# Moving 56 elementwise adds from VectorE to GpSimd in a one-core transformer layer

## The chip, the core and the metric

The kernel runs on one core of a Trainium2 chip. The engines are named as in the profile: PE (TensorE, matmul) with PEld (its weight loads), DVE (VectorE), ACT (ScalarE), POOL (GpSimd) and SP (SyncE, which here issues nearly all DMAs). Each engine executes its own instructions strictly in their order in the program, and waits on semaphores for the others. The metric is the device time of one execution in microseconds (us); lower is better.

## What is computed

One layer of a streaming encoder on `x` (2048 tokens of 1024 float32 values): a token mixer, cross-attention into 256 memory tokens, and a SwiGLU feed-forward net, each between two RMS norms and with a residual.

```python
u = rms_norm(h, g_mix_pre)
qa, ka, va, qh, fh, ih, gh = jnp.split(u @ w_in, IN_SPLITS, axis=-1)
y = jnp.concatenate([swa_with_sinks(qa, ka, va, sinks),        # sliding-window attention
                     hgrn2(qh, fh, ih, gh, lb, onorm)], -1) @ w_out
h = h + rms_norm(y, g_mix_post)
u = rms_norm(h, g_x_pre)
y = cross_attention(u, rms_norm(mem, g_mem), wq_x, wk_x, wv_x, wo_x)
h = h + rms_norm(y, g_x_post)
u = rms_norm(h, g_ffn_pre)
y = (jax.nn.silu(u @ w_gate) * (u @ w_up)) @ w_down
h = h + rms_norm(y, g_ffn_post)
```

## The kernel before, in words

**Products.** All float32 products are made of three matmuls each on operands split into a high and a low part: hi*hi, hi*lo, lo*hi (lines 1131 to 1133). The big products are in addition done by a seven-product scheme on 2x2 blocks (`seven`, steps 1, 5, 6, 3, 7, 2, 4). It needs sums and differences of the blocks of both operands. A token operand's blocks and sums are tiles named `S` (128x512) and `sum`; a weight operand's are tiles named `T`. Each is split by `split2`: the high part is copied by ACT (line 987) or by POOL (line 989), the low part is a subtraction on DVE (line 990) of two tiles in SBUF. A step of `seven` is 12 matmuls; `phases` makes the `S` two steps ahead, into five buffers.

**Sums of the weights ahead of time.** The four combined weight blocks of the chain (`CHAIN`, keys 5, 7, 6, 4) are made once, ahead of the stage that needs them, and kept in DRAM. `sums` (line 1418) makes the DRAM tile and a generator `combined` (line 1027), which for two halves of the inner dimension loads two blocks of 128x1024, lets three steps go by, adds or subtracts them on DVE (line 1034) and stores the result. That is 8 adds for each weight. They run beside the stage before: `out_s` (sums of `w_out`) beside the sliding-window attention (line 228), `qk_s` beside the out projection, `vo_s` beside the scores, `u_s` and `d_s` in the feed-forward net. The tiles come from small pools: `u` and `x` (2 and 3 buffers) for `out_s`, one `extra` tile with `row` or `gain` tiles for the others.

**Stages, in order of time.** The input projection; the sliding-window attention with the HGRN recurrence and the rest of the input projection between them (`swa`, `hgrn`, `in_proj`); the folding of the cross-attention weights into a query-key matrix `qk_d` and a value-output matrix `vo_d`; then `phases` over the jobs of `jobs` (line 1441): the out projection (`mixed_block`), the scores (`score_block`), the values (`value_block`), then gate, up and down of the feed-forward net. Each of the first three jobs has 8 blocks of 256 tokens.

**What follows a block.** `mixed_block` and `value_block` have an `after` generator that is drawn a little at each of the following steps. In `mixed_block` (line 1539): the reciprocal norm on POOL (`rstds`, lines 1515 to 1519, three tiny instructions), a scaling on DVE (line 1557), the residual add of the rows of `x` (line 1558, two of 128x1024 for a block), the store of the new rows, squares on ACT (line 1504), another reciprocal norm, and transposes on DVE (line 1398). `value_block` is alike: scaling (1630), residual add of the rows of `h1_d` (1634, two for a block), store, squares, reciprocal norm, scaling (1643), transposes on PE (1390). In `score_block` POOL makes a tiny product `x_mr` (line 1590) for each half row, which ACT's exponentials (line 1592) wait for.

**The order of the work** on each engine is fixed when the program is built: the scheduler places the instructions by priority and by its own timeline, and each engine then keeps to that order. `behind()` ties the instructions traced in it behind the last marked ones of ACT and DVE, each only on that same engine.

Of the kernel before, what the change touches and what calls it, by code (L numbers as in the profile page):

```python
# [15 lines left out]
ALU = mybir.AluOpType  # L16
# [32 lines left out]
class Layer:  # L49
# [144 lines left out]
    def mix(self):  # L194
        tc, I = self.tc, self.I
        kw = dict(reuse_waits="tile")
        with contextlib.ExitStack() as left:
            def pool(name, at, **k):
                return at.enter_context(tc.tile_pool(name=name, bufs=1, **k, **kw))

            self.mc = pool("mc", left)
            self.r_x = self.cst.tile([P, NT], F32, name="r_x")
            with (
                tc.tile_pool(name="t1", bufs=3, **kw) as self.ts,
                tc.tile_pool(name="t2", bufs=3, **kw) as self.tb,
                tc.tile_pool(name="s1", bufs=2, side="right", **kw) as self.st_pool,
                contextlib.ExitStack() as at,
            ):
                self.banks(at, "ps1", **MOST)
                self.raws = 3  # L210
                u = self.in_first()
            self.banks(left, "ps2", **FOUR)
            self.hg = pool("hg", left)
            self.wp = pool("wp", left)
            self.io = pool("io", left)
            with tc.tile_pool(name="sw", bufs=1, side="right", **kw) as self.sw:
                self.zero_tiles()
                swa = self.swa(range(NT), lambda n: "st" if n < NPB else "sth")
                hgrn = self.hgrn(range(NPB), "h")
                cols = self.in_proj(1, u)  # L220
                next(cols)
                for _ in range(NPB + 1):
                    next(swa)
                    next(hgrn)
                    next(cols)
                for _ in hgrn:
                    pass
                self.out_sums, side = self.sums("out_s", self.w_out, 4, lambda: self.io_tile("u"), lambda: self.io_tile("x"))
                side = side()
                next(side)  # L230
                pairs = self.hgrn(range(NPB, NT), "gt")
                for i, _ in enumerate(swa, NPB + 2):
                    next(cols)
                    if i == NT + 1 - 0:
                        next(pairs)
                    for _ in range(4):
                        next(side, None)
                for _ in cols:
                    pass
            phases = self.phases(self.jobs(), None, lambda: self.io_tile("z"))  # L240
            with tc.tile_pool(name="xp", bufs=1, side="right", **kw) as self.xp:
                fold = self.fold_cross()
                for _ in range(2):
                    next(fold)
                for i, _ in enumerate(pairs, 1):
                    for _ in range(2):
                        next(fold)
                    if 2 <= i < 10:
                        next(phases)
                for _ in fold:  # L250
                    pass
            left.close()
            with (
                tc.tile_pool(name="t3", bufs=3, **kw) as self.ts,
                tc.tile_pool(name="t4", bufs=3, **kw) as self.tb,
                tc.tile_pool(name="s3", bufs=2, side="right", **kw) as self.st_pool,
                contextlib.ExitStack() as at,
            ):
                self.banks(at, "ps3", **MOST)
                self.raws = 4  # L260
                for _ in phases:
                    pass
# [761 lines left out]
                keep[key] = src  # L1024
            yield lambda a=a, b=b, t=t, o=o: split(a, b, t, o)

    def combined(self, get, nk, dst):

        nc = self.nc
        halves = [(0, (nk + 1) // 2), ((nk + 1) // 2, nk)]  # L1030
        for a, b in halves:
            def put(key, t, o, op):
                with self.behind():
                    nc.vector.tensor_tensor(t, t, o, op)
                self.store(dst[self.CHAIN.index(key), :, a * 512:b * 512], t.rearrange("p k d -> p (k d)"))

            for x, y, key in (((0, 1), (0, 0), 5), ((1, 1), (0, 1), 7), (None, (0, 0), 6), (None, (1, 0), 4)):
                if x:
                    t = get(0, *x, a, b - a)
                o = get(1, *y, a, b - a)  # L1040
                for _ in range(3):
                    yield
                if key == 4:
                    put(4, o, t, ALU.subtract)
                else:
                    put(key, t, o, ALU.add if key == 6 else ALU.subtract)
                yield
# [367 lines left out]
            p = P if i else 64  # L1415
            self.load(d, self.I["w_out"][r:r + p * n, j * 512:(j + 1) * 512].rearrange("(k p) d -> p k d", p=p))

    def sums(self, name, src, nk, *tiles):

        dst = self.tc.dram_tile([4, P, nk * 512], F32, name=name)  # L1420

        def get(which, i, j, k0, n):
            t = tiles[which]().rearrange("p (k d) -> p k d", d=512)[:, :n]
            src(t, i, j, k0, n)
            return t

        return dst, lambda: self.combined(get, nk, dst)

    def token_sums(self, a, o, n):

# [10 lines left out]
    def jobs(self):  # L1441
        I = self.I

        def weights(src, r0, nk):
            return lambda t, i, j, k0, n: self.load(
                t, src[r0 + (i * nk + k0) * P:r0 + (i * nk + k0 + n) * P, j * 512:(j + 1) * 512]
                .rearrange("(k p) d -> p k d", p=P))

        def ffn_u(b):
            return lambda t, i, j, k0, n: self.load(  # L1450
                t, self.u_d[4 * i + k0:4 * i + k0 + n, :, b * TB + j * 512:b * TB + (j + 1) * 512]
                .rearrange("k p t -> p k t"))

        def kinds(blocks, n=0, last="p"):
            return [("p" if i < n else last if i == len(blocks) - 1 else "s",) + b for i, b in enumerate(blocks)]

        def sums(name, src, nk, other=None):
            return self.sums(name, src, nk, self.extra_tile, other or self.gain_tile)

        def in_turn(*what):  # L1460
            return lambda: itertools.chain.from_iterable(w() for w in what)

        qk, vo = weights(self.qk_d, 0, 4), weights(self.vo_d, 0, 4)
        down = [(weights(I["w_down"], f0 * P, nk), f0, nk) for f0, nk in ((0, 3), (6, 4), (14, 4))]
        qk_s, vo_s = sums("qk_s", qk, 4, self.row_tile), sums("vo_s", vo, 4)
        u_s = sums("u_s", ffn_u(1), 4)
        self.u0_s = self.tc.dram_tile([4, P, 4 * 512], F32, name="u0_s")
        d_s = [sums(f"d_s{c}", src, nk) for c, (src, _, nk) in enumerate(down)]
        jobs = [(self.w_out, 4, kinds([self.mixed_block(n) for n in range(0, NT, 2)], 1), self.out_sums, {1: [qk_s[1]]}),
                (qk, 4, kinds([self.score_block(n) for n in range(0, NT, 2)]), qk_s[0], {1: [vo_s[1]]}),  # L1470
                (vo, 4, kinds([self.value_block(n) for n in range(0, NT, 2)]), vo_s[0], {})]
        for b in range(NB):
            beside = {2: [in_turn(*(d[1] for d in d_s))]} if b else {4: [u_s[1]]}
            jobs.append((ffn_u(b), 4, kinds([blk for f in range(0, NFF, 2) for blk in self.hidden_blocks(b, f)], 0, "s"),
                         u_s[0] if b else self.u0_s, beside))
        for c, (src, f0, nk) in enumerate(down):
            jobs.append((src, nk, kinds([self.down_block(c, f0, nk, n) for n in range(0, NT, 2)], 0, "s"), d_s[c][0], {}))

        return jobs
# [59 lines left out]
    def mixed_block(self, n):  # L1539
        nc = self.nc  # L1540
        y, x, ss = {}, [], []
# [11 lines left out]
        def after():  # L1553
            r = self.rstds(ss[0])
            s2 = self.small("q_s", 4)
            for i in range(2):
                nc.vector.scalar_tensor_tensor(y[i], y[i], r[:, i:i + 1], self.g_mix_post, ALU.mult, ALU.mult)
                nc.vector.tensor_tensor(y[i], y[i], x[i], ALU.add)
                self.store(self.h1_d[(n + i) * P:(n + i + 1) * P, :], y[i])
                yield  # L1560
            yield
# [48 lines left out]
    def value_block(self, n):  # L1610
        nc = self.nc
        y, ss, u, o = {}, [], {}, {}
# [12 lines left out]
        def after():  # L1625
# [5 lines left out]
            yield  # L1631
            yield
            for i in range(2):
                nc.vector.tensor_tensor(y[i], y[i], x[i], ALU.add)
                self.store((self.out if n < NT - 2 else self.h2_d)[(n + i) * P:(n + i + 1) * P, :], y[i])
                yield
            for i in range(2):
# [153 lines left out]
```

## Time and profile before

| | |
|---|---|
| median of 3 runs | 2554.41 us (2552.43 to 2555.48) |
| the profiled execution | 2550.01 us, its span 2548.3 us |
| PE busy | 2504.8 us, 98% |
| PEld busy | 2092.8 us, 82% |
| DVE busy | 1792.1 us, 70% |
| ACT busy | 1261.6 us, 50% |
| POOL busy | 364.6 us, 14% |
| mean granted clock of PE | 0.997 |

Times in the views are counted from the start of the span. Busy time is the time in which an instruction of the engine was running. An instruction that stands in its engine's queue and waits for a semaphore counts as idle; the views name in brackets what ended such a wait. Matmuls overlap each other, so the listed 390 ns of one is longer than the distance of two.

### The profile page before, as it was taken

How to read it: one execution, taken by the hardware profiler on the slowest of the kernel's cores; microseconds unless marked ns; L12 is line 12 of the kernel's file. 1: busy time of each engine (PE TensorE's matmuls, PEld its weight loads, DVE VectorE, ACT ScalarE, POOL GpSimd, SP SyncE). 2: the span in 40 equal slices, each digit the busy share in tenths (PEclk: the TensorE clock that was granted, in tenths of full speed). 3: DMA queues.
4: the chain of work that ended last, by engine and by line, in shares of the span. 5: the costliest groups of instructions: out<-in, count | busy, mean ns of one | idle time of the engine just before them, and what ended most of it. 6: DMA issues, size and time to landing. Idle time of an engine off the chain costs nothing.

```text
span 2548.3 us, 34324 instructions
## 1 busy us (share of the span) xinstructions
PE 2504.8 (98%) x12006; PEld 2092.8 (82%) x12006; DVE 1792.1 (70%) x2871; ACT 1261.6 (50%) x2635; POOL 364.6 (14%) x540
## 2 busy tenths in 40 slices
PE   9999999999999999999999999999999999999998
PEld 8878888877997778878878888888888888878886
DVE  8885488987556989988876555576566557574766
ACT  5553466655555566566753333353333335443543
POOL 4231234321311112102200000000000000000022
PEclk9999999999999999999999999999999999999999
DMA  6455655865887996867954522254465434564786
GB/s 201 146 165 178 192 154 170 230 204 146 259 292 275 316 335 189 274 206 226 333 200 146 177 91 87 74 203 148 160 210 195 144 117 159 180 188 106 228 177 151
DMA packets 387885, 486.33 MB, mean 191 GB/s; under 512 B 22272, under 2 KB 283392, under 8 KB 387712
## 3 DMA queue, kind: packets, MB, share of 16 engines
q1 hardware_dynamic: 381664, 462.12, 55.9%
q0 software_dynamic: 6048, 22.02, 5.0%
q8 instruction: 94, 1.54, 0.2%
q14 instruction: 79, 0.65, 0.1%
HBM read 317.34 MB, written 166.72 MB: 190 GB/s over the span
## 4 chain that ended last, share of the span: by engine, by line
PE 51%; DVE 2%; DMA 1%; issue 1%; ACT 1%; POOL 0%; SPq 0%; DVEq 0%; POOLq 0%; ACTq 0%
PE psm L1133 17%; PE psm L1131 17%; PE psm L1132 17%; DVE T L990 0%; DVE S L990 0%; ACT junk L1504 0%; PE pss L1390 0%; DMA out_dram<-row 0%; DMA row<-d_s 0%; DMA row<-in_w_down_dram 0%; DMA u_d<-row 0%; DMA sraw<-in_w_gate_dram 0%; DVE sum L1106 0%; ACT S L987 0%; ACT T L987 0%
## 5 line engine op out<-in xcount | busy, mean ns | idle before, releaser
L1131 PE MATMUL psm<-T,S 128*128 128x512 f32 x2680 | 1034.1, 390 | 13.3 <-ACT part L1146 7.2
L1132 PE MATMUL psm<-T,S 128*128 128x512 f32 x2680 | 1042.3, 390 | 4.0 <-DVE T L990 3.9
L1133 PE MATMUL psm<-T,S 128*128 128x512 f32 x2680 | 1029.4, 389 | 4.1 <-DVE S L990 4.1
L1131 PEld LDWEIGHTS psm<-T,S 128*128 128x128 f32 x2680 | 503.0, 188 | 125.9 <-ACT part L1146 11.9
L1132 PEld LDWEIGHTS psm<-T,S 128*128 128x128 f32 x2680 | 503.2, 188 | 110.5 <-DVE T L990 7.3
L1133 PEld LDWEIGHTS psm<-T,S 128*128 128x128 f32 x2680 | 503.1, 188 | 110.6 <-DVE S L990 6.3
L987 ACT ACTIVATE S<-sum 128x512 fp32r<-128x512 f32 (+1 forms) x370 | 224.0, 620 | 371.5 <-PE psm L1133 267.3
L990 DVE TENSOR_TENSOR S<-sraw,S 128x512 fp32r<-128x512 f32 (+1 forms) x315 | 211.5, 679 | 218.8 <-ACT S L987 215.8
L1146 ACT ACTIVATE part<-psm 128x512 f32<-128x512 f32 x285 | 168.6, 596 | 251.9 <-PE psm L1133 230.9
L990 DVE TENSOR_TENSOR S<-sum,S 128x512 fp32r<-128x512 f32 (+1 forms) x388 | 257.4, 673 | 42.1 <-ACT S L987 38.3
L987 ACT ACTIVATE S<-sraw 128x512 fp32r<-128x512 f32 (+1 forms) x300 | 184.7, 618 | 110.8 <-PE psm L1133 106.0
L1537 POOL DMA_DIRECT2D y_d<-row x16 | 14.1, 879 | 1077.9 <-DVE row L1721 1027.6
L990 DVE TENSOR_TENSOR T<-row,T 128x1024 fp32r<-128x1024 f32 (+1 forms) x112 | 131.0, 1183 | 30.2 <-ACT T L987 29.2
L157 PE MATMUL psg<-u,whi 128*128 128x512 f32 x320 | 128.3, 401 | 0.0
L158 PE MATMUL psg<-u,wlo 128*128 128x512 f32 x320 | 127.6, 399 | 0.0
L156 PE MATMUL psg<-u,whi 128*128 128x512 f32 x320 | 127.5, 399 | 0.0
L1504 ACT ACTIVATE junk<-row 128x512 f32<-128x512 f32 x160 | 99.6, 624 | 40.6 <-DVE row L1526 20.6
L987 ACT ACTIVATE T<-row 128x1024 fp32r<-128x1024 f32 (+1 forms) x112 | 113.3, 1031 | 7.5 <-DMA row<-d_s 4.3
L1672 DVE TENSOR_TENSOR row<-psm,part 128x512 f32<-128x512 f32 x66 | 43.7, 687 | 66.9 <-PE psm L1133 66.9
L1681 DVE TENSOR_TENSOR part<-psm,part 128x512 f32<-128x512 f32 x66 | 43.8, 687 | 60.1 <-PE psm L1133 59.8
L1721 DVE TENSOR_TENSOR row<-psm,part 128x512 f32<-128x512 f32 x72 | 49.1, 688 | 49.5 <-PE psm L1133 49.4
L814 ACT ACTIVATE S<-S,w_mn 128x256 f32<-128x256 f32 (+1 forms) x128 | 63.0, 496 | 29.6 <-DVE w_mn L810 29.2
(363 smaller groups left out, 3562.2 us busy)
## 6 DMA issues: line engine op xcount, KB each, us to landing
sraw<-in_w_gate_dram SPq DMA_DIRECT2D x44, 512.0 KB, 3.6
sraw<-in_w_up_dram SPq DMA_DIRECT2D x44, 512.0 KB, 3.7
hid_d<-row SPq DMA_DIRECT2D x44, 512.0 KB, 2.7
sraw<-hid_d SPq DMA_DIRECT2D x32, 512.0 KB, 4.2
sraw<-in_w_in_dram SPq DMA_DIRECT2D x44, 256.0 KB, 4.0
z_d<-pair SPq DMA_DIRECT2D x20, 512.0 KB, 3.4
raw<-in_w_in_dram SPq DMA_DIRECT2D x20, 512.0 KB, 4.8
z_d<-z SPq DMA_DIRECT2D x20, 512.0 KB, 4.0
```

The source lines that it names most:

```text
L156: nc.tensor.matmul(ps, ah, bh, start=(i == 0), stop=False)
L157: nc.tensor.matmul(ps, ah, bl, start=False, stop=False)
L158: nc.tensor.matmul(ps, al, bh, start=False, stop=(i == n - 1))
L814: nc.scalar.activation(s[:, r, o:], s[:, r, o:], AF.Exp, bias=mn[:, i:i + 1], scale=-1.0, accum_out=den[:, i:i + 1])
L987: self.nc.scalar.activation(hi, raw, AF.Copy)
L990: self.nc.vector.tensor_tensor(lo, raw, f32(hi), ALU.subtract)
L1131: nc.tensor.matmul(ps, s[:, 0, k, :], t[:, 0, k, :], start=st, stop=False, **kw)
L1132: nc.tensor.matmul(ps, s[:, 0, k, :], t[:, 1, k, :], start=False, stop=False, **kw)
L1133: nc.tensor.matmul(ps, s[:, 1, k, :], t[:, 0, k, :], start=False, stop=sp, **kw)
L1146: nc.scalar.activation(t, ps, AF.Copy)
L1504: self.nc.scalar.activation(junk, a, AF.Square, scale=float(D) ** -0.5, accum_out=to)
L1721: nc.vector.tensor_tensor(d, a, b, ALU.add)
```

## The change

Three groups of adds, 56 instructions of 128x1024 each, are issued on POOL instead of DVE:

- line 1558, the residual of the out projection: 16 adds
- line 1634, the residual of the values: 16 adds
- line 1034, for `out_s`, `qk_s` and `vo_s`: 8 adds each, 24

The sums `u_s` and `d_s` stay on DVE. No operand, no tile and no load is changed.

```diff
-                self.out_sums, side = self.sums("out_s", self.w_out, 4, lambda: self.io_tile("u"), lambda: self.io_tile("x"))
+                self.out_sums, side = self.sums("out_s", self.w_out, 4, lambda: self.io_tile("u"), lambda: self.io_tile("x"),
+                                                 on=self.nc.gpsimd)
...
-    def combined(self, get, nk, dst):
+    def combined(self, get, nk, dst, on):
...
                 with self.behind():
-                    nc.vector.tensor_tensor(t, t, o, op)
+                    on.tensor_tensor(t, t, o, op)
...
-        return dst, lambda: self.combined(get, nk, dst)
+        return dst, lambda: self.combined(get, nk, dst, on or self.nc.vector)
...
-        qk_s, vo_s = sums("qk_s", qk, 4, self.row_tile), sums("vo_s", vo, 4)
+        qk_s, vo_s = sums("qk_s", qk, 4, self.row_tile, on=self.nc.gpsimd), sums("vo_s", vo, 4, on=self.nc.gpsimd)
...
-                nc.vector.tensor_tensor(y[i], y[i], x[i], ALU.add)
+                nc.gpsimd.tensor_tensor(y[i], y[i], x[i], ALU.add)
                 self.store(self.h1_d[(n + i) * P:(n + i + 1) * P, :], y[i])
...
-                nc.vector.tensor_tensor(y[i], y[i], x[i], ALU.add)
+                nc.gpsimd.tensor_tensor(y[i], y[i], x[i], ALU.add)
                 self.store((self.out if n < NT - 2 else self.h2_d)[(n + i) * P:(n + i + 1) * P, :], y[i])
```

More of the change, by code (lines that the diff above doesn't have):

```diff
@@ L1025, in resident @@
             yield lambda a=a, b=b, t=t, o=o: split(a, b, t, o)
-    def combined(self, get, nk, dst):
-        nc = self.nc
+    def combined(self, get, nk, dst, on):
         halves = [(0, (nk + 1) // 2), ((nk + 1) // 2, nk)]
@@ L1416, in w_out, with sums @@
             self.load(d, self.I["w_out"][r:r + p * n, j * 512:(j + 1) * 512].rearrange("(k p) d -> p k d", p=p))
-    def sums(self, name, src, nk, *tiles):
+    def sums(self, name, src, nk, *tiles, on=None):
         dst = self.tc.dram_tile([4, P, nk * 512], F32, name=name)
@@ L1455, in kinds, with sums @@
             return [("p" if i < n else last if i == len(blocks) - 1 else "s",) + b for i, b in enumerate(blocks)]
-        def sums(name, src, nk, other=None):
-            return self.sums(name, src, nk, self.extra_tile, other or self.gain_tile)
+        def sums(name, src, nk, other=None, **at):
+            return self.sums(name, src, nk, self.extra_tile, other or self.gain_tile, **at)
         def in_turn(*what):
```

## The prediction, made before the changed kernel ran

> **What bounds the kernel now.** I read the page's first part, then the busy time of the stages in which adds are moved (each row gives the stretch, then busy time of PE, PEld, DVE, ACT and POOL with the instructions counted, clock, DMA share and GB/s).
>
> ```profile
> PE 2504.8 (98%) x12006; PEld 2092.8 (82%) x12006; DVE 1792.1 (70%) x2871; ACT 1261.6 (50%) x2635; POOL 364.6 (14%) x540
> ```
>
> ```profile
> 440.00:526.00 86.00, 84.73 (x465) 71.42 (x464) 77.02 (x165) 52.43 (x140) 28.73 (x40) 1.00 0.86 249
> 800.00:955.00 155.00, 149.31 (x649) 120.75 (x647) 138.69 (x177) 96.51 (x211) 25.61 (x50) 1.00 0.93 311
> 955.00:1105.00 150.00, 148.88 (x655) 122.81 (x655) 140.42 (x264) 92.02 (x218) 27.38 (x36) 1.00 0.79 238
> 1105.00:1300.00 195.00, 187.03 (x864) 151.90 (x865) 164.96 (x206) 129.13 (x277) 31.67 (x48) 1.00 0.78 261
> ```
>
> PE is the bound everywhere. In these four stages (attention with `out_s`, out projection, scores, values) it idles 86.00 - 84.73 = 1.27, then 5.69, 1.12 and 7.97 us: 16.1 us together. No change of DVE's work can win more than that. DVE is the busiest helper: 90%, 89%, 94% and 85% of these stages, so it has 9.0, 16.3, 9.6 and 30.0 us of idle time left.
>
> Next, whom PE waited for. First the waits of PE in the out projection, then in the scores, then in the values (sum, times, longest):
>
> ```profile
> PE psm L1133 <- DVE S L990: 1.4, 2, 1.2
> PE psm L1132 <- DVE T L990: 0.6, 1, 0.6
> ```
>
> ```profile
> PE psm L1132 <- DVE T L990: 1.4, 1, 1.4
> ```
>
> ```profile
> PE psm L1133 <- DVE S L990: 2.7, 2, 1.6
> PE psm L1132 <- DVE T L990: 1.9, 4, 0.8
> ```
>
> So 8.0 us of PE's idle time end with a low part that DVE made late. That is what the change can remove, and also what it can make longer.
>
> **What is removed from DVE.** The groups by line and shape, cut to the stages (count | busy, mean ns | idle before them and what ended it):
>
> ```profile
> L1034 DVE TENSOR_TENSOR u<-u,x 128x1024 f32<-128x1024 f32 x6 | 7.3, 1214 | 3.0 <-DMA out_s<-u 2.8 <-issue 0.3
> ```
>
> ```profile
> L1558 DVE TENSOR_TENSOR row<-row,row 128x1024 f32<-128x1024 f32 x16 | 19.1, 1216 | 0.0
> L1034 DVE TENSOR_TENSOR extra<-extra,row 128x1024 f32<-128x1024 f32 x6 | 7.3, 1213 | 3.0 <-issue 1.9 <-DMA qk_s<-extra 1.1
> ```
>
> ```profile
> L1034 DVE TENSOR_TENSOR extra<-extra,g 128x1024 f32<-128x1024 f32 x6 | 7.3, 1216 | 3.3 <-DMA extra<-vo_d 3.3
> ```
>
> ```profile
> L1634 DVE TENSOR_TENSOR row<-row,row 128x1024 f32<-128x1024 f32 x16 | 19.1, 1217 | 0.0
> ```
>
> Of the 24 sums these rows show 18; the other 6 have the same shape. 56 adds of 1.217 us are 68 us of DVE. Instructions on DVE overlap a little (16 take 19.1 us), so one costs its queue 1.13 to 1.20 us; in a row of two I count 1.13 (2.35 for both, below). Besides, 3.0 + 3.0 + 3.3 = 9.3 us go in which DVE stood at the head of its queue waiting for the load of a sum. Nearly all of this lies beside PE's work and is worth nothing. One wait is not. First DVE, then PE:
>
> ```profile
> 881.41 1.22 DVE L1034 TENSOR_TENSOR extra<-extra,row 128x1024 f32<-128x1024 f32 x1 [1.08 <-DMA qk_s<-extra]
> 882.55 0.68 DVE L1106 TENSOR_TENSOR sum<-sum,sraw 128x512 f32<-128x512 f32 x1
> 883.15 0.68 DVE L990 TENSOR_TENSOR S<-sraw,S 128x512 fp32r<-128x512 f32 x1
> ```
>
> ```profile
> 883.89 0.50 PE L1133 MATMUL psm<-T,S 128*128 128x512 f32 x1 [1.25 <-DVE S L990]
> ```
>
> Without the add, its 1.08 us of waiting and its 1.13 us go from ahead of `S`, 2.2 us against PE's 1.25: **-1.25 us**. Next late there is ACT, which waits for PE itself.
>
> **What the same add costs on POOL.** No POOL add of 128x1024 is in the trace; the nearest row is one of half the size with two inputs (minimum, median, maximum in ns):
>
> ```profile
> L914 POOL TENSOR_TENSOR W<-W,G x16: 1042/1046/2005, 254.2 to 717.1; 128x512 f32<-128x512 f32 x16
> ```
>
> So about 2 x 1.04 = 2.1 us alone (estimate; its ends are the 1.04 of half the size and 4.0, twice the maximum). POOL has the time: 56 x 2.1 = 118 us against some 470 idle in these stages. But why is the maximum 2005? POOL, then DVE, around that instruction:
>
> ```profile
> 359.32 2.00 POOL L914 TENSOR_TENSOR W<-W,G 128x512 f32<-128x512 f32 x1
> ```
>
> ```profile
> 358.15 2.33 DVE L734 TENSOR_TENSOR_SCAN u<-reset,x 128x512 f32<-128x512 f32 x2
> 360.52 1.36 DVE L771 SCALAR_TENSOR_TENSOR qs<-qd,qs 64x512 fp32r<-64x512 f32 x1
> ```
>
> ```profile
> L771 DVE SCALAR_TENSOR_TENSOR qs<-qd,qs x32: 687/690/1579, 275.0 to 581.9; 64x512 fp32r<-64x512 f32 x32
> ```
>
> The scans (two inputs in SBUF) end at 360.48, and POOL's add, issued at 359.32, ends at 361.32: it worked 0.84 us after them. DVE's next instruction, also with two SBUF inputs, takes 1.36 instead of 0.69: it stood 0.67 us until POOL let go. They exclude each other. For twice the length I take 2 x 0.84 = 1.7 us during which DVE stands (1.3 from 2 x 0.67, 2.1 from the whole duration). Where DVE works without a pause on two-input instructions, an add on POOL thus costs DVE 1.7 instead of 1.13: **0.57 us more, not 1.13 less** (0.2 to 1.0). Where DVE has a pause or reads PSUM, the 1.13 are won, mostly where PE does not wait.
>
> [...]
>
> **Where that meets a wait of PE.** (1) The end of the out projection:
>
> ```profile
> 950.79 1.22 DVE L1558 TENSOR_TENSOR row<-row,row 128x1024 f32<-128x1024 f32 x1
> 951.93 1.22 DVE L990 TENSOR_TENSOR T<-row,T 128x1024 fp32r<-128x1024 f32 x1
> 953.06 0.69 DVE L990 TENSOR_TENSOR S<-sraw,S 128x512 fp32r<-128x512 f32 x1
> 953.66 1.22 DVE L1558 TENSOR_TENSOR row<-row,row 128x1024 f32<-128x1024 f32 x1
> 954.80 1.22 DVE L990 TENSOR_TENSOR T<-row,T 128x1024 fp32r<-128x1024 f32 x1
> ```
>
> ```profile
> 953.20 0.50 PE L1132 MATMUL psm<-T,S 128*128 128x512 f32 x1 [0.55 <-DVE T L990]
> 956.07 0.50 PE L1132 MATMUL psm<-T,S 128*128 128x512 f32 x1 [1.44 <-DVE T L990]
> ```
>
> DVE has no pause and nearly all of it has two inputs. Two adds stand ahead of the `T` that PE waits for: 2 x 0.57 = **+1.1 us** (between -2.0, if POOL gets its turn only after that `T`, and +2.0).
>
> (2) The values, where token sums follow the residual. SP, DVE, PE:
>
> ```profile
> 1196.47 1.48 SPq L78 DMA_DIRECT2D out_dram<-row  x2
> ...
> 1199.82 0.67 SPq L78 DMA_DIRECT2D u_d<-row  x1
> ```
>
> ```profile
> 1195.22 2.35 DVE L1634 TENSOR_TENSOR row<-row,row 128x1024 f32<-128x1024 f32 x2
> ...
> 1206.44 0.69 DVE L1432 TENSOR_TENSOR row<-row 128x512 f32<-128x512 f32 x1 [2.26 <-DMA u_d<-row]
> ```
>
> ```profile
> 1211.40 0.50 PE L1133 MATMUL psm<-T,S 128*128 128x512 f32 x1 [1.63 <-DVE S L990]
> ```
>
> SP stands at the stores of the rows until the adds are done (1196.4 and 1195.22 + 2.35 = 1197.57), then comes to the store of `u_d`; DVE's token sum waits for that store to land, and the `S` behind it makes PE wait. On POOL the second add ends about 1.8 us later (start at 1195.3 after the `S` that DVE has in hand, 1.7, up to 0.7 for a DVE instruction between, 1.7 = 1199.4): **+1.8 us**. In the changed program three more stores precede that `u_d` store, but one `S` less stands behind the token sum; so I keep 1.8, between -1.6 (the wait gone) and +5. This is the queue where the move counts most: every residual store has SP's next `sraw` load behind it, but those loads are for the block after (a block takes 150 / 8 = 19 us), so a shift of 2 us is hidden there; without that cover it would be 2 us for each of 16 blocks.
>
> (3) The last block of the values:
>
> ```profile
> 1288.68 0.50 PE L1132 MATMUL psm<-T,S 128*128 128x512 f32 x1 [0.47 <-DVE T L990]
> ```
>
> Right ahead of that `T` DVE does one residual add: **+0.6 us**. In the other pairs PE does not wait on DVE, and DVE's pauses take the excess.
>
> (4) On POOL's own queue stand, behind an add that waits for its load: the three tiny norm instructions, the high parts of some weights, and in the scores `x_mr`, for which ACT waits already (in that stage from 1000 on):
>
> ```profile
>   ACT row L1592: 20.9, 11
> ```
>
> ACT's copies of `S` queue behind those exponentials. But `S` is made two steps ahead, 24 matmuls of 148.88 / 655 = 0.227 us, that is 5.4 us, and PE idles almost nowhere in that stage. Cost 0; without the cover 7 adds x 2.1 us = 15. In the attention I cost the exchange at 0 as well: PE idles 1.27 us there, half of DVE's work reads PSUM, and the scheduler reorders all engines (-1 to +2).
>
> **The sum.** -1.25 + 1.1 + 1.8 + 0.6 = +2.3 us: 2550.0 + 2.3 = 2552.3 us for the profiled execution. The median before is 2554.41, 4.4 us above that execution, so the forecast is **2556.7 us**, 0.1% slower. A measurement of this kernel can tell about 0.2% (5.1 us) from no change: that is 2549.3 to 2559.5.
>
> **Rivals.** *DVE's relief decides.* POOL takes its adds in DVE's pauses, and the waits on DVE's `S` and `T` go: -8.0 us and about 1 in the attention, **2545.4 us**. For it: 65 us of DVE's idle time in the four stages and the 9.3 us of head-of-queue waits. Against it: 56 adds want 95 us of exclusive access, and where PE waits there are no pauses. Chance 0.21.
>
> *The exclusion decides (slower).* In the out projection DVE is at 89%, and 24 adds each take 0.57 us more of it: 13.7 us against 16.3 us idle. Much of that idle time is DVE waiting for PE or ACT, so it can't be used. If nearly every grant to POOL meets a ready two-input instruction, DVE bounds that stage: +13.7 - 1.25 = 12.4, **2566.8 us**. It decides as soon as more than about half of the grants do so. [...] Chance 0.19.
>
> *POOL's queue decides (slower).* `x_mr` or the high part of a weight comes late behind adds that wait for loads: half of the 14.6 us above, **about 2562 us**. Chance 0.15.
>
> That the change does not do what it says is excluded: the built program has 56 more instructions on POOL, on just these lines.
>
> **How the numbers follow.** Forecast 0.45, rivals 0.21, 0.19 and 0.15. Faster by over 0.2%: 0.21; within: 0.45; slower: 0.34. The range goes from the first rival to the second, 2545 to 2567.
>
> **What would show it.** The 56 adds on POOL at about 2.1 us, up to 3 where DVE is busy; DVE instructions with two SBUF inputs at up to 1.7 us above their 0.69 or 1.22 beside them, those with a PSUM input unchanged; no wait before 883.9, longer ones at the end of the out projection and at the token sums. Wrong would be: PE's idle time in the four stages under 11 us or above 24, or a PE wait on something that stands behind POOL.

## The result: 2.2% slower, and the profile after

The changed kernel takes 2610.43 us (median of 4 runs, 2606.12 to 2611.78), the kernel before in the same session 2554.36 (2552.43 to 2555.48): ratio 1.0221, 95% interval 1.0208 to 1.0233. The forecast was 2556.7 us, with a range of 2545 to 2567. The profiled execution takes 2609.64 us (span 2607.9, granted clock 0.990 instead of 0.997).

First the page's busy times after the change:

```profile
PE 2525.1 (97%) x12006; PEld 2103.6 (81%) x12006; DVE 1825.5 (70%) x2815; ACT 1257.3 (48%) x2635; POOL 532.6 (20%) x596
```

Two things are odd here. DVE has lost 56 adds (68 us) and is busy 33 us *longer* than its 1792.1. And PE, with the same 12006 matmuls, is busy 20.3 us longer than its 2504.8. Now the four stages, cut at the same matmuls as in the prediction (stretch, its length, then busy time of PE, PEld, DVE, ACT, POOL, and the granted clock):

```profile
438.20:532.90 94.70, 87.96 (x464) 73.91 (x463) 75.55 (x164) 53.42 (x146) 45.75 (x51) 0.96 0.84 222
812.90:988.80 175.90, 156.59 (x649) 124.71 (x648) 158.84 (x155) 95.21 (x210) 98.69 (x73) 0.95 0.82 268
988.80:1152.50 163.70, 155.12 (x657) 125.61 (x655) 141.98 (x252) 91.24 (x218) 50.78 (x46) 0.97 0.72 220
1152.50:1360.80 208.30, 191.32 (x867) 154.19 (x866) 179.27 (x189) 128.73 (x276) 84.48 (x64) 0.98 0.76 248
```

Against 86, 155, 150 and 195 us the stages are 8.7, 20.9, 13.7 and 13.3 us longer, 56.6 in all. PE's idle time in them is 6.7, 19.3, 8.6 and 17.0 us, together 51.6 instead of 16.1 (+35.5). The other 21.1 us are PE's *busy* time, and the clock column gives most of the reason: 0.95 to 0.98 instead of 1.00. The span is 59.6 us longer: another 6.0 us lie between the attention and the out projection, where nothing was moved (532.9 to 812.9, 280.0 us instead of 274.0), and what stands before and after is 3.0 us shorter.

Whom PE waits for, in the out projection, the scores and the values:

```profile
PE psm L1133 <- DVE S L991: 11.5, 5, 5.4
```

```profile
PE psm L1131 <- ACT S L988: 5.3, 1, 5.3
```

```profile
PE pss L1390 <- DVE row L1643: 5.0, 2, 4.0
PE psm L1132 <- DVE T L991: 3.8, 4, 2.0
```

There are a few long waits where there were short ones: `S` had cost 1.4 us in the out projection, the longest 1.2. Next some groups of the moved adds on POOL (busy time, mean ns of one):

```profile
L1558 POOL TENSOR_TENSOR row<-row,row 128x1024 f32<-128x1024 f32 x16 | 57.0, 3582 | 17.6 <-DVE row L1557 10.5 <-DMA h1t_d<-row 7.0
L1034 POOL TENSOR_TENSOR extra<-extra,row 128x1024 f32<-128x1024 f32 x6 | 16.5, 2746 | 83.7 <-DMA row<-in_x_dram 68.4 <-DMA row<-qk_d 11.8 <-DMA qk_s<-extra 2.9
L1034 POOL TENSOR_TENSOR g<-g,extra 128x1024 f32<-128x1024 f32 x2 | 4.8, 2389 | 2.2 <-DMA g<-vo_d 2.2
```

Hardly disturbed, an add takes 2.39 us; in the out projection 3.58, since it waits for DVE inside itself. The longest of them shows it (minimum, median and maximum in ns, then the first and last start):

```profile
L1558 POOL TENSOR_TENSOR row<-row,row x16: 2376/3371/10322, 816.9 to 991.5; 128x1024 f32<-128x1024 f32 x16
```

The add of 10.32 us begins at 981.20. DVE makes one two-input instruction after another up to 989.27, all of them at their usual length, and POOL's add ends at 991.52, 2.25 us after DVE's last. Here POOL stood, and not DVE.

DVE's groups in the out projection, after the change and then before it:

```profile
L991 DVE TENSOR_TENSOR S<-sraw,S 128x512 fp32r<-128x512 f32 x25 | 36.6, 1474 | 1.4 <-ACT S L988 1.4
L1526 DVE TENSOR_TENSOR row<-psm,part 128x512 f32<-128x512 f32 x18 | 12.3, 685 | 9.5 <-issue 6.7 <-PE psm L1133 1.9 <-ACT part L1146 0.9
```

```profile
L990 DVE TENSOR_TENSOR S<-sraw,S 128x512 fp32r<-128x512 f32 x24 | 16.3, 684 | 4.3 <-ACT S L987 4.3
L1526 DVE TENSOR_TENSOR row<-psm,part 128x512 f32<-128x512 f32 x18 | 12.3, 682 | 1.9 <-ACT part L1146 0.9 <-DMA h1t_d<-row 0.9
```

The subtraction for `S` has two SBUF inputs: 684 ns became 1474. The sum with one input in PSUM (`psm`) kept its 685. One such moment in full (start, duration, engine, line):

```profile
835.41 2.87 POOL L1034 TENSOR_TENSOR extra<-extra,row 128x1024 f32<-128x1024 f32 x1 [11.81 <-DMA row<-qk_d]
835.97 2.85 DVE L991 TENSOR_TENSOR S<-sum,S 128x512 fp32r<-128x512 f32 x1
838.75 0.68 DVE L1106 TENSOR_TENSOR sum<-sum,sraw 128x512 f32<-128x512 f32 x1
839.35 0.68 DVE L991 TENSOR_TENSOR S<-sraw,S 128x512 fp32r<-128x512 f32 x1
840.08 0.50 PE L1133 MATMUL psm<-T,S 128*128 128x512 f32 x1 [3.54 <-DVE S L991]
```

POOL's add begins at 835.41 and ends at 838.28. DVE's `S`, issued at 835.97, ends 0.54 us after it: 2.85 us instead of 0.69. DVE then makes one sum and the next `S`, the one that PE has been waiting for since 836.54: 3.54 us. Undisturbed it would have been there at about 837.9, so DVE was late even before this add. What comes next for PE, in three stretches of 3.41 us:

```profile
837.98:841.39 3.41, 1.31 (x6) 1.09 (x7) 3.25 (x5) 0.82 (x2) 3.15 (x6) 1.00 1.11 353
841.39:844.80 3.41, 3.41 (x10) 2.64 (x9) 1.08 (x2) 0.63 (x1) 1.02 (x3) 0.50 1.05 292
844.80:848.20 3.40, 3.40 (x16) 2.77 (x15) 3.40 (x2) 1.11 (x2) 3.07 (x2) 1.00 0.15 57
```

In the second stretch PE never waits, and yet starts 10 matmuls instead of 16: the clock is 0.50. So the stop of 3.54 us is paid for with up to another 1.7 us (estimate: half of the 3.41 us). In the whole trace there are 14 such stretches after the change and 2 before (without the one at the very end). PE was working in 39.7 us of the 14 and in 6.7 us of the 2; at half clock half of that is lost, so about (39.7 - 6.7) / 2 = 16.5 us of PE's 20.3 us of added busy time come from the clock (estimate). Where the other 4 us come from stays open. PE's idle time (all its gaps over 0.15 us) went from 33.8 to 73.6 us, +39.8.

### The profile page after: what moved, and what is told of

It is laid out like the page before. It is cut to its first block, busy times and chain, and to the rows that moved or that the text cites. A ratio compares the mean times of both kernels' runs of the same rounds, so it can differ in the third digit from the quotient of the medians.

```text
span 2607.9 us, 34359 instructions
## 1 busy us (share of the span) xinstructions
PE 2525.1 (97%) x12006; PEld 2103.6 (81%) x12006; DVE 1825.5 (70%) x2815; ACT 1257.3 (48%) x2635; POOL 532.6 (20%) x596
## 4 chain that ended last, share of the span: by engine, by line
PE 51%; DVE 5%; DMA 4%; issue 2%; ACT 1%; POOL 1%; SPq 0%; DVEq 0%; POOLq 0%; ACTq 0%
PE psm L1131 17%; PE psm L1133 17%; PE psm L1132 17%; DVE S L991 1%; DVE T L991 1%; ACT junk L1504 1%; DMA h1t_d<-row 1%; DVE sum L1106 1%; DMA extra<-vo_d 0%; DVE row L1398 0%; POOL row L1558 0%; DMA g<-vo_d 0%; DVE row L1526 0%; DMA out_dram<-row 0%; DMA row<-vo_s 0%
## 5 line engine op out<-in xcount | busy, mean ns | idle before, releaser
L991 DVE TENSOR_TENSOR S<-sraw,S 128x512 fp32r<-128x512 f32 (+1 forms) x315 | 246.6, 792 | 213.3 <-ACT S L988 210.3
L991 DVE TENSOR_TENSOR S<-sum,S 128x512 fp32r<-128x512 f32 (+1 forms) x388 | 281.9, 735 | 44.5 <-ACT S L988 40.8
L991 DVE TENSOR_TENSOR T<-row,T 128x1024 fp32r<-128x1024 f32 (+1 forms) x112 | 141.3, 1277 | 29.6 <-ACT T L988 27.8
```

The costliest lines, as they stand in the source:

```text
L991: self.nc.vector.tensor_tensor(lo, raw, f32(hi), ALU.subtract)
```

## The experiments

Theory A: an add on POOL and a two-input instruction on DVE exclude each other; where PE needs the result of the latter, it stops, and stops of that length also cost it clock. The rivals: B, POOL's in-order queue (adds that wait for loads hold up what stands behind them); C, the scheduler's new order on all engines; D, the longer time of the add itself, for what depends on it. Each run is compared with the kernel before on the same chip.

### Each stage alone

The five moves, split by the stage in which they run; this is the edit that leaves only the attention's (line 1634 goes back like 1558; the others leave only theirs). The expectations speak of a drift: by how much a matmul starts later than the same one in the trace of before.

```diff
-        qk_s, vo_s = sums("qk_s", qk, 4, self.row_tile, on=self.nc.gpsimd), sums("vo_s", vo, 4, on=self.nc.gpsimd)
+        qk_s, vo_s = sums("qk_s", qk, 4, self.row_tile, on=self.nc.vector), sums("vo_s", vo, 4, on=self.nc.vector)
...
-                nc.gpsimd.tensor_tensor(y[i], y[i], x[i], ALU.add)
+                nc.vector.tensor_tensor(y[i], y[i], x[i], ALU.add)
```

> Only the 8 adds for out_s run on GpSimd, the other 48 on VectorE. Theory A (an add on GpSimd and a two-input instruction on VectorE exclude each other; where TensorE waits for that VectorE instruction it stops 2 to 5 us, and such a stop costs it a stretch at half clock besides): the drift of the changed kernel up to the end of the folding, +13 us, comes back, about 2567. Theory B (GpSimd's queue: an add waiting for its load holds up what stands behind it): also about 2567, with the stops ending on high parts or w_se that GpSimd made late. Theory C (the scheduler made another order on all engines, and that order is slower): any number, and the four groups do not add up to +56. Forecast: no difference, 2554.

> Only the 16 residual adds of the out projection and the 8 adds for qk_s run on GpSimd. Theory A: +19 us as in the drift of the changed kernel over this stage, about 2573, with stops of 2.5 to 5 us behind S and half-clock stretches behind them. Theory B: under +5, since only the three tiny norm instructions stand behind the adds. Theory C: any number.

> Only the 8 adds for vo_s run on GpSimd. Theory A: few two-input instructions in this stage have TensorE behind them, +4, about 2558. Theory B: x_mr waits behind adds that wait for their loads, ACT waits for x_mr, TensorE for ACT's S: +13, about 2567. Theory C: any number.

> Only the 16 residual adds of the values run on GpSimd. Theory A: +14 us as in the drift of the changed kernel over this stage, about 2568. Theory B: +5 at most (the token sums' chain over the stores). Theory C: any number.

| adds on POOL | ratio (95%) | us | DVE busy |
|---|---|---|---|
| `out_s` (8) | 1.0052 (1.0035 to 1.0069) | +13 | 1786.9 |
| `qk_s` and line 1558 (24) | 1.0107 (1.0092 to 1.0122) | +27 | 1813.1 |
| `vo_s` (8) | 1.0044 (1.0029 to 1.0059) | +11 | 1794.1 |
| line 1634 (16) | 1.0056 (1.0041 to 1.0071) | +14 | 1808.2 |

Every move costs time by itself. The sum, +66 with an interval of about 8 us, is a little more than the +56 of all together. Theory A had expected +13, +19, +4 and +14 for the four rows, theory B +13, under 5, +13 and at most 5. B alone can't explain +27 where only norms stand behind the adds, nor the +14 of the values. In the attention the two expect the same. In the scores +11 is nearer to B.

### What it is about the add

The changed kernel, with the adds replaced by two memsets of the result (nothing read), by two products by 1.0 (one SBUF input), or by nothing; and the kernel before with its adds kept on DVE and an idle add behind each on POOL.

The edits are shown for line 1558; 1034 and 1634 go alike.

```diff
-                nc.gpsimd.tensor_tensor(y[i], y[i], x[i], ALU.add)
+                [nc.gpsimd.memset(y[i], 0.0) for _ in range(2)]
```

```diff
-                nc.gpsimd.tensor_tensor(y[i], y[i], x[i], ALU.add)
+                [nc.gpsimd.tensor_scalar(y[i], y[i], 1.0, 1.0, ALU.mult, ALU.mult) for _ in range(2)]
```

```diff
-                nc.gpsimd.tensor_tensor(y[i], y[i], x[i], ALU.add)
+                nc.vector.tensor_tensor(y[i], y[i], x[i], ALU.add)
+                nc.gpsimd.tensor_tensor(x[i], y[i], x[i], ALU.add)
```

> The changed kernel with each of the 56 adds replaced by two memsets of its first operand on GpSimd (the sums and residuals are left out; loads, stores and waits stay). GpSimd is as long busy and waits for the same loads, but reads no operand. Theory A (exclusion, then the clock): VectorE's two-input instructions are back at 0.69 us, no stops, 2545 to 2555. Theory B (GpSimd's queue): x_mr still waits for the loads ahead of it, 2565 to 2580. Theory C (another order on all engines): about 2600.

> The changed kernel with each of the 56 adds replaced by two in-place products by 1.0 on GpSimd (one SBUF input each; sums and residuals are left out). Theory A, if any GpSimd instruction that reads SBUF excludes: about 2600 as in the changed kernel. Theory A, if only one with two inputs does: 2550 to 2558 as with the memsets.

> The changed kernel with the 56 adds left out altogether, loads and stores kept. This is what VectorE's relief is worth by itself: theories A and B 2542 to 2550. Theory C: above 2555.

> The kernel before with VectorE's 56 adds kept, and behind each an idle add of the same size on GpSimd, into the operand that is no longer needed; nothing but that buffer's release waits for it. Theory A (exclusion, then the clock): VectorE's two-input instructions stand about 95 us in all as in the changed kernel, 2595 to 2615. Theory D (the add's own latency, 2.4 to 3.6 us instead of 1.2, makes what depends on it late): nothing depends on these, 2553 to 2560.

| in place of the add | ratio (95%) | us, median | DVE busy | POOL busy | half-clock stretches |
|---|---|---|---|---|---|
| nothing | 0.9996 (0.9985 to 1.0006) | 2551.84 | 1731.2 | 358.3 | 2 |
| two memsets | 1.0005 (0.9995 to 1.0015) | 2555.95 | 1739.7 | 459.0 | 6 |
| two one-input products | 1.0095 (1.0080 to 1.0110) | 2577.44 | 1779.3 | 529.1 | 5 |
| the add (the change) | 1.0221 (1.0208 to 1.0233) | 2610.43 | 1825.5 | 532.6 | 14 |
| adds on DVE, idle adds on POOL | 1.0244 (1.0228 to 1.0260) | 2615.73 | 1875.1 | 559.4 | 14 |

DVE's low parts of `S` in the out projection with the memsets:

```profile
L991 DVE TENSOR_TENSOR S<-sraw,S 128x512 fp32r<-128x512 f32 x25 | 16.9, 685 | 7.6 <-ACT S L988 7.6
```

With memsets the 685 ns are back and the loss is gone, although POOL keeps 94 us of its 168 us of new work and waits for the load of its first operand as before (17.8 us for `extra` from `vo_d`; after the change 15.0). Since the order of the work was new here too, C doesn't explain the loss as a whole. A memset doesn't wait for the second operand's load (17.0 us for `g` from `vo_d` after the change), so B isn't tested by this alone. The idle adds decide between A and D: no instruction needs their result, only what writes over their operands waits for them, and the loss is about that of the change. D falls. POOL's tiny norm instructions do stand behind the idle adds too, so this run doesn't exclude B.

The one-input products came out between the two expectations (2600 if any reading instruction excludes, 2550 to 2558 if only one with two inputs does). They do exclude, but cost DVE about half (48.1 us against 94.3, from the DVE column). Each of them is also shorter than an add (1.12 us undisturbed), so whether one input or the shorter length makes the difference stays open.

The first row gives what the exclusion costs DVE: 1825.5 - 1731.2 = 94.3 us for 56 adds, **1.68 us each**, and 48.1 us with one-input products. It also shows what the relief is worth. The stages without the adds, cut at the same matmuls (the second row is everything between the attention and the out projection), and then that part before the change:

```profile
439.20:527.90 88.70, 85.09 (x464) 71.08 (x463) 72.41 (x173) 54.71 (x151) 24.46 (x40) 1.00 0.86 244
527.90:807.70 279.80, 268.21 (x1706) 239.33 (x1705) 160.66 (x312) 150.23 (x364) 51.32 (x79) 0.99 0.71 227
807.70:961.20 153.50, 149.62 (x648) 122.16 (x647) 116.74 (x157) 98.62 (x215) 26.38 (x50) 0.99 0.98 330
961.20:1109.70 148.50, 148.50 (x657) 122.94 (x655) 128.69 (x249) 90.32 (x214) 25.46 (x36) 1.00 0.69 210
1109.70:1301.10 191.40, 185.99 (x866) 151.97 (x865) 148.11 (x190) 129.53 (x277) 33.78 (x48) 1.00 0.82 271
```

```profile
526.00:800.00 274.00, 266.47 (x1708) 238.30 (x1706) 167.77 (x325) 153.84 (x374) 50.78 (x80) 0.99 0.71 229
```

The last three stages win 1.5, 1.5 and 3.6 us, 6.6 together; PE's waits for DVE's `S` and `T` in them fall from 8.0 to 3.8 us. The first two stretches lose 2.7 and 5.8. Theories A and B had expected 2542 to 2550 of this run; by its interval even free adds would win at most some 4 us.

### The order in the attention

```diff
-        return dst, lambda: self.combined(get, nk, dst, on or self.nc.vector)
+        return dst, lambda: self.combined(get, nk, dst, None if name == "out_s" else self.nc.vector)
...
-                    on.tensor_tensor(t, t, o, op)
+                    if on is not None:
+                        on.tensor_tensor(t, t, o, op)
```

This is the kernel before without the 8 adds of `out_s`, all others on DVE.

> The kernel before with the 8 adds of out_s left out and nothing put on GpSimd. Theory C for the attention alone (the scheduler's other order there costs about 6 us, whatever takes the adds): drift of +5 to +9 at the end of the folding, 2558 to 2562. If the order costs nothing: drift of 0 to +2.5 there, 2552 to 2556.

The ratio is 1.0026 (1.0012 to 1.0039): +7 us, for work taken away and nothing put in its place. The drift at the end of the folding was +4.3 us, just under what C expected, where four programs with an unchanged attention have +1.6 to +2.9. So the runs speak for C in the attention, with some part of that stage's +13. The tables above say the same: the attention and the stretch behind it are 8.7 + 6.0 = 14.7 us longer in the changed kernel, and 2.7 + 5.8 = 8.5 us of that are there without any add. The runs don't divide the rest between the exclusion and the queue.

### Shorter adds, and POOL's queue

The first edit cuts the adds in four (1034 and 1634 alike), the second ties those of the weights' sums (in `behind` and `mark`).

```diff
-                nc.gpsimd.tensor_tensor(y[i], y[i], x[i], ALU.add)
+                for q in range(4):
+                    nc.gpsimd.tensor_tensor(y[i][:, q * 256:(q + 1) * 256], y[i][:, q * 256:(q + 1) * 256],
+                                            x[i][:, q * 256:(q + 1) * 256], ALU.add)
```

```diff
-            for e in (mybir.EngineType.Activation, mybir.EngineType.DVE):
+            for e in (mybir.EngineType.Activation, mybir.EngineType.DVE, mybir.EngineType.Pool):
```

> The changed kernel with each of the 56 adds cut into four of 128x256 on GpSimd. Theory A, if VectorE gets its turn between two quarters: it stands at most 0.7 us at a time instead of up to 2.9, TensorE's stops stay under 1.5 us and the half-clock stretches go: 2560 to 2580. Theory A, if GpSimd takes the next quarter first: about 2610. Theories B and C: about 2610, since the queue and its waits are the same.

> The changed kernel with the adds for the sums of weights tied behind the last marked instruction of GpSimd too (as they are for ACT and VectorE), which moves them later in GpSimd's queue, in the scores behind several x_mr; nearly nothing else moves. Theory B: the waits of ACT for x_mr and the stop at 1065 go, 10 us or more faster, 2595 to 2600 in all if half of the loss lies there. Theory A alone: the same exclusions at other places, 2605 to 2615.

Quarters: 1.0136 (1.0119 to 1.0153), some 20 us better than the change, though 10 us above the range expected. DVE stands 1783.9 - 1731.2 = 53 us instead of 94; its longest `S` in the four stages is 1.30 us instead of 2.90, and half-clock stretches fall from 14 to 7. DVE does get its turn between two quarters. But PE's stops didn't stay under 1.5 us as expected: the longest in the four stages is 5.3 us, in the scores, where PE waits for ACT's `S`.

Tied: 1.0199 (1.0180 to 1.0218), about 5 us better if at all, since the intervals overlap. Most of POOL's waits for the loads of `qk_s` and `vo_s` are gone, as this row shows against the 83.7 us above (68.4 of which are a single early wait):

```profile
L1034 POOL TENSOR_TENSOR extra<-extra,row 128x1024 f32<-128x1024 f32 x6 | 16.7, 2780 | 8.9 <-issue 3.8 <-DMA qk_s<-extra 3.1 <-DMA extra<-qk_d 2.0
```

So the loads ahead of POOL's adds are a small part. But the run did not free ACT in the scores, as theory B had expected of it. Here is how long ACT waits there for `x_mr`, before, after the change and tied:

```profile
ACT row L1592 <- POOL x_mr L1590: 25.2, 14, 6.4
```

```profile
ACT row L1592 <- POOL x_mr L1590: 48.5, 19, 6.9
```

```profile
ACT row L1592 <- POOL x_mr L1590: 52.4, 23, 8.2
```

By the traces 18.3 us of the 48.5 are 5 waits for an `x_mr` that stood behind an add on POOL, and 13.2 us of the 52.4, also 5; in nearly all the others POOL itself had waited for DVE's `x_mx`, which `x_mr` reads. So how the loss of the scores divides between the exclusion and POOL's queue stays open. One of the waits in the changed kernel:

```profile
1064.49 2.61 POOL L1034 TENSOR_TENSOR extra<-extra,g 128x1024 f32<-128x1024 f32 x1 [5.42 <-DMA g<-vo_d]
1067.08 0.98 POOL L1590 TENSOR_SCALAR x_mr<-x_mx,r_x 128x2 f32<-128x2 f32 x2
1067.84 0.60 ACT L1592 ACTIVATE row<-row,x_mr,r_x 128x256 f32<-128x256 f32 x1 [5.92 <-POOL x_mr L1590]
1070.86 0.79 PE L1131 MATMUL psm<-T,S 128*128 128x512 f32 x1 [5.28 <-ACT S L988]
```

The add waits 5.42 us for its load, `x_mr` stands behind it, ACT waits 5.92 us for `x_mr` and only then copies the `S` that PE has been waiting for.

### Another way to take the adds off DVE

```diff
-                nc.gpsimd.tensor_tensor(y[i], y[i], x[i], ALU.add)
+                self.add(y[i], self.I["x"], n + i)
```

All sums are on DVE as before; the 32 residual adds are accumulating DMAs (line 1634 with `h1_d`), and the loads of the rows are dropped.

> A version that would take the 32 residual adds off VectorE without GpSimd's arithmetic: they are done by accumulating DMAs that GpSimd issues, and the rows of x and h1 aren't loaded beforehand. With the adds left out altogether the stages behind the folding gained about 7 us. If the relief is what counts, 2547 to 2551. If the accumulating transfer (issue and landing some 3 us) comes late for the stores, squares and transposes behind it, or its issue on GpSimd holds VectorE up too, 2556 to 2580.

It takes 2580.68 us, 1.0106 (1.0091 to 1.0121). DVE's two-input instructions keep their length here (the subtractions for `S` from `sraw` take 689 ns in the mean of the whole trace, as before the change). What is late is the transfer (first row: issues, KB, median us to landing; no run shows the expected 3 us for an accumulating transfer: in the trace of before, those of 512 KB take 5.1 to 7.7 us). SP stands at the stores of the rows until it has landed (60.6 us in all in the out projection), the next `sraw` loads stand behind them, and DVE's sums wait up to 12.0 us for these (second row). PE waits for the `S` made from them (third row), and in the values for the rows (fourth row):

```profile
row<-in_x_dram POOLq DMA_DIRECT2D x16, 512.0 KB, 8.7
```

```profile
DVE sum L1106 <- DMA sraw<-h1t_d: 19.4, 2, 12.0
PE psm L1133 <- DVE S L991: 12.8, 4, 5.8
PE pss L1390 <- DVE row L1641: 8.8, 3, 6.8
```

An add that needs 8.7 us instead of 1.2 does reach PE. No version that ran is faster than the kernel before.

## Why the prediction was wrong

**The exclusion was seen, and its price for DVE was right on average.** 1.7 us of DVE standing for an add were forecast, from one POOL instruction of half the size; measured are 1.68. That they agree so closely is partly luck: 1.7 was meant for an add beside a DVE without a pause, and 1.68 is the mean over all 56, in which a single DVE instruction stood for up to 2.2 us, or for nothing, as at 981.20. The add itself takes 2.39 us undisturbed, not 2.1. The forecast took the exclusion from a single DVE instruction (1.36 us instead of 0.69); the table shows it over all 56 adds: memsets, which read nothing, cost DVE 8.5 us, the adds 94.

**The step that failed is the sentence "In the other pairs PE does not wait on DVE, and DVE's pauses take the excess".** The prediction netted the 1.7 us against the removed 1.13 and charged the difference, 0.57, at two places where PE waited already. But a stand isn't spread over the stage. It falls on one instruction, as at 835.97, and lasts up to 2.2 us; what counts is how far ahead of PE that instruction is made. In the out projection that is nothing: the `S` for which PE stopped at 836.54 stood two instructions behind the one that was hit. A DVE that is busy 89% *and* works just in time has no pause to give. The rival "the exclusion decides" had the mechanism and sized it in the same way, as DVE's throughput: +12.4 for a stage that became 20.9 us longer, and nothing for the others.

**A cost that no step contained: the clock.** Some 16 of the 60 us are matmuls at half clock behind long stops (the estimate above). The trace of before had it (two stretches, the granted clock 0.997), but no step asked what a stop does to PE afterwards.

**Point by point.** -1.25 at 883.9: the wait of 1.25 is gone there, but around it PE now stops 2.54 us at 879.67 and 5.39 us at 908.50. Place (1), +1.1 for the end of the out projection: PE's waits for `T` there fell from 2.0 us to 0.9. POOL got its turn only after these `T` (the add at 981.20). That is the case that the prediction had as the low end. The stage lost its 20.9 at other places. Place (2), token sums: the chain was right and its size not far off. The prediction put each add at 1.7 us, less than its own estimate of 2.1, so 4.1 us for the pair; the pair took 6.18 us from 1244.85 on. PE's stop was to grow from 1.63 by 1.8 to 3.4 us; it became 4.0, at the transposes and no longer at an `S`:

```profile
1262.81 0.69 DVE L1432 TENSOR_TENSOR row<-row 128x512 f32<-128x512 f32 x1 [2.76 <-DMA u_d<-row]
1266.77 1.07 PE L1390 MATMUL pss<-ident,row 128*128 128x128 f32 x8 [4.02 <-DVE row L1643]
```

Place (3), +0.6 for the last block of the values: its wait of 0.47 is gone, because POOL's adds (from 1344.51 on) again got their turn only after that `T`; an earlier `T` now stops PE for 2.02. Place (4), POOL's queue at 0: the stop of 5.28 us at 1065 is what was called covered. POOL's waits for loads are worth some 5 us or less by the tied version; what the queue costs through `x_mr` stays open. Attention at 0: it lost 8.7 and the stretch behind it 6.0; about half of this shows without any add. The two signs named as "wrong would be" both came: idle time of 51.6 us in the four stages against a bound of 24, and a PE wait on something behind POOL.

**The rival "DVE's relief decides"** was wrong even about its best case: with no adds at all the kernel takes as long as before. About half of the waits on `S` and `T` go (4.2 of 8.0 us) and the three stages get 6.6 us shorter, but the attention and what follows it give that back.

## What to carry to other kernels

POOL was no free second DVE here: each add of 128x1024 on POOL made DVE stand 1.68 us on average, more than the 1.13 to 1.20 us of doing it there. Price such a move by the longest single stand and by how far ahead of PE the hit instruction is made, not by a mean against an engine's idle share. And before moving work off an engine that isn't the bound, leave the work out altogether in one run: here that showed a gain of nothing.

## What the runs showed of the hardware

**The half clock of PE came in stretches of 3.41 us.** In all 14 traces the half-clock stretches lie on a grid of 3.413 us whose phase differs from run to run (in the changed kernel those that begin at 496.64 and at 1268.06 are 226 of its steps apart). I cut each trace between 0.1 and 2.5 ms by its own grid, 9842 stretches. Behind a stretch in which PE was idle 1.9 us or more, the next ran at half clock 59 times of 59. With 1.4 to 1.9 us of idle time it did 19 times of 66; below 1.4 us 12 times of 9717, and 11 of these 12 came right behind another half-clock stretch. So in these traces a single stop under 1.4 us mostly cost only itself. One of 2 to 3.4 us brought a half-clock stretch in 26 of 44 cases, and with it up to 1.7 us more (the estimate above); all 23 longer ones did. Where the grid cuts a stop goes with it: after the change the stop of 2.54 us at 879.67 lies within one stretch, and the next ran at half clock; the one of 2.02 us at 1342.12 is cut in two, and none did. This relation is read from the traces; no run changed the clock by itself.

**What excludes what.** On DVE, instructions with one input in PSUM (line 1526) and one-input reductions and transposes (1588, 1398) kept their length: 0.67 to 0.69 us in the mean of each group, before and after the change and with quarters, memsets, products, idle adds, no adds and accumulating DMAs. Those with two SBUF inputs were stretched, most by adds, less by one-input products on POOL, and not by memsets: the subtractions for `S` from `sraw` took 811, 734 and 689 ns in the mean of the whole trace, and 688 with the adds left out; in DVE's whole busy time the products cost about half of what the adds did (48.1 us of 94.3). What memsets do stretch are scalings with one SBUF input in the attention (line 826 from 438 to 700 us: 13 of 68 took over 0.55 us instead of 0.35, with the adds left out 1 of 68; in the whole trace the 120 of that line keep DVE busy for 46.1 us instead of 37.4); beside the adds one such scaling took 2.49 us. Which side stands is not fixed: at 835.97 a DVE instruction stood 2.2 us for POOL's add, at 981.20 POOL's add took 10.32 us while DVE's kept their length.
